# The first layer's pooling mixer: one more root, the band constants on another queue, and an order by hand for three engines

## The chip, the cores and the metric

The program runs on one core of one Trainium2 chip. The metric is device time in microseconds (us) of one execution, from start to end; three executions of the kernel before took 1045.97, 1046.10 and 1046.62 us.

## What is computed

The reference is a decoder trunk of two layers on 512 tokens of width 1024, behind which 16 learned meta rows are put in front (528 rows). Layer 0 mixes tokens by multi-scale causal pooling, layer 1 by stick-breaking attention; each layer ends with a SwiGLU network of width 2816. The change touches the pooling mixer alone:

```python
def rmsnorm(x, g):
    xf = x.astype(jnp.float32)
    y = xf * lax.rsqrt(jnp.mean(xf * xf, axis=-1, keepdims=True) + EPS)
    return (y * g.astype(jnp.float32)).astype(x.dtype)

def pool_mixer(h, w, scale):
    ...
    for g, win in enumerate(POOL_WINDOWS):          # windows 2, 4, 8, 16
        xg = hf[..., g * POOL_GROUP:(g + 1) * POOL_GROUP]
        cs = jnp.cumsum(xg, axis=1)
        lag = jnp.pad(cs[:, :-win], ((0, 0), (win, 0), (0, 0)))
        cnt = jnp.minimum(pos + 1, win).astype(jnp.float32)[None, :, None]
        outs.append((cs - lag) / cnt - xg)
    pooled = jnp.stack(outs, axis=2).astype(h.dtype)
    mixed = jnp.einsum('blgc,gcd->blgd', pooled, w).reshape(B, L, D_MODEL)
    return mixed * scale
```

## The kernel before

Matrices are held transposed, as eight chunks of 128 channels by 528 rows (`hT`). Each fp32 operand of a large matmul is split into a rounded part and the rest, so that a product is three matmuls (`mm3`, line 108): the ScalarE writes the rounded part, the VectorE subtracts.

The opening (from line 180) has four input tiles `xt[0..3]` of 128 tokens and one tile `mt` of the 16 meta rows, each 1024 wide, and goes through these steps:

- **Squares and roots.** The sum of squares of a row is made by ScalarE for tiles 0 and 2 (line 219) and by VectorE for the meta rows and tiles 1 and 3 (line 221). VectorE adds the epsilon (line 223), ScalarE takes the reciprocal root (line 137), VectorE refines it with three small operations (lines 138, 140, 141). There are two such roots: one for tiles 0, 1 and the meta rows together, one for tiles 2 and 3.
- **Split.** ScalarE writes the normalised tile rounded (`ah`, line 228), VectorE the rest (`al`, line 229), ScalarE the meta rows (`am`, line 231).
- **Bands.** The moving average is a matmul against a banded matrix. VectorE copies the constants `band_raw` into the zeroed `band` (line 232); GpSimd has set the zeros.
- **Pooling.** TensorE first runs 30 matmuls of zeros (line 238). Then it makes 16 pooled tiles: eight chunks of the first half of the rows (tiles 0 and 1 and the meta rows: lines 251, 252, 254) and eight of the second half (tiles 1, 2 and 3: six matmuls each). Each takes one of eight PSUM banks, and a bank is free for the second half only when ScalarE has written `ph` (line 257) and VectorE `pl` (line 258) from it.
- **Weights and mixing.** `pool_w` arrives in two loads and is split into `pw0`, `pw1` (lines 94 and 99). 16 products `mix` follow (line 108), each added to `hT` by VectorE (`h`, line 269). After a chunk's second half `norm.chunk` prepares the operands of the first feed-forward layer: `f0uh` and `f0sq` on ScalarE, `f0ul` and the sum of `f0sq` on VectorE.

The first feed-forward product (`pp`, line 108) takes over the PSUM banks of the opening, and waits for the last `h`. Every engine runs its instructions in one fixed order; the framework's scheduler chooses it from the order of the source and its own estimates. Loads go out on two queues: SP's (nearly all) and ScalarE's (`mt` and `gains`); a queue's loads share eight completion semaphores in turn, and SP waits before reusing one.

Of the kernel before, what the change touches and what calls it, by code (L numbers as in the profile page):

```python
# [7 lines left out]
F32 = mybir.dt.float32  # L8
F32R = mybir.dt.float32r
BF16 = mybir.dt.bfloat16  # L10
AF = mybir.ActivationFunctionType
ALU = mybir.AluOpType

P = 128
D = 1024
KC = D // P
SEQ = 512
META = 16
# [4 lines left out]
EPS = 1e-6  # L23
# [3 lines left out]
BOFF = 144  # L27
# [20 lines left out]
def f32(ap):  # L48
    return ap.bitcast(F32)
# [3 lines left out]
def trunk(ctx: ExitStack, tc: tile.TileContext, x, meta, x_t, gain, pool_w, w_qkv, w_o, w_gate, w_up, w_down,  # L53
          final_gain, c_ident, c_band, c_mband, c_mask, out):

    nc = tc.nc
# [8 lines left out]
    @contextmanager  # L65
    def phase(name, **bufs):
        with tc.tile_pool(name=name, bufs=1, space=bass.MemoryType.PSUM) as pool:
            psum["pool"], psum["bufs"] = pool, bufs
            yield

    def ps(name, tag, banks=1):

        shape = [P, 512] if banks == 1 else [P, banks, 512]
        return psum["pool"].tile(shape, F32, tag=tag, name=name, bufs=psum["bufs"][tag])
# [9 lines left out]
    def wsplit(v, name, eng=None, src=None):  # L84


        n, m = v.shape[1], v.shape[2]
        step = max(1, 512 // m)
        his, los = [], []
        for j in range(0, n, step):  # L90
            w = min(step, n - j)
            hi = main.tile([P, step, m], F32R, tag="whi", name=f"{name}h{j}", bufs=NW)[:, :w]
            lo = main.tile([P, step, m], F32R, tag="wlo", name=f"{name}l{j}", bufs=NW)[:, :w]
            nc.scalar.copy(hi, v[:, j:j + w])  # L94
            if src is not None:
                nc.scalar.activation(lo, v[:, j:j + w], AF.Copy, scale=-1.0)
                nc.gpsimd.dma_start(out=lo, in_=src[:, j:j + w], accum_op=ALU.add)
            else:
                (eng or nc.vector).tensor_tensor(out=lo, in0=v[:, j:j + w], in1=f32(hi), op=ALU.subtract)
            his += [hi[:, i] for i in range(w)]  # L100
            los += [lo[:, i] for i in range(w)]
        return his, los
# [31 lines left out]
    def rstd_of(parts, r, t):  # L134

        for ss, sl in parts:
            nc.scalar.activation(r[:, sl], ss, AF.Abs_reciprocal_sqrt, scale=1.0 / D)
        nc.vector.tensor_tensor(out=t, in0=r, in1=r, op=ALU.mult)
        for ss, sl in parts:
            nc.vector.scalar_tensor_tensor(t[:, sl], ss, -0.5 / D, t[:, sl], op0=ALU.mult, op1=ALU.mult)  # L140
        last_rstd[:] = [nc.vector.scalar_tensor_tensor(r, t, 1.5, r, op0=ALU.add, op1=ALU.mult).ins]
        return r
# [40 lines left out]
    with tc.tile_pool(name="start", bufs=1) as sp, phase("ps0", one=8):  # L183
        nc.scalar.activation(sp.tile([P, 1], F32, name="table"), ones[:, 0:1], AF.Abs_reciprocal_sqrt)
        xt = [sp.tile([P, D], F32, name=f"x{i}") for i in range(4)]
        mt = sp.tile([META, D], F32, name="mt")
        band_raw = sp.tile([P, 4, 144], F32, name="bandr")
        mband = sp.tile([P, 4, 32], F32, name="mband")
        nc.sync.dma_start(out=xt[0], in_=x[0, 0:P, :])
        nc.scalar.dma_start(out=mt, in_=meta)  # L190
        nc.sync.dma_start(out=xt[1], in_=x[0, P:2 * P, :])
        nc.scalar.dma_start(out=gains, in_=gain)
        for i in (2, 3):
            nc.sync.dma_start(out=xt[i], in_=x[0, i * P:(i + 1) * P, :])
        nc.sync.dma_start(out=band_raw, in_=c_band)
        nc.sync.dma_start(out=mband, in_=c_mband)
        pwr = [wraw(pool_w[0, :, k * P:(k + 1) * P, :].rearrange("g p d -> p g d"), f"pwr{k}") for k in range(2)]
        for c in range(KC):
            nc.sync.dma_start(out=hT[c], in_=x_t[c * P:(c + 1) * P, :])
        nc.sync.dma_start(out=consts, in_=c_ident)  # L200
        nc.sync.dma_start(out=masks, in_=c_mask)

        band = sp.tile([P, 4, BAND], F32R, name="band")
        nc.gpsimd.memset(f32(band), 0.0)
        ah = [sp.tile([P, D], F32R, name=f"ah{i}") for i in range(4)]
        al = [sp.tile([P, D], F32R, name=f"al{i}") for i in range(4)]
        am = sp.tile([P, D], F32, name="am")
        nc.gpsimd.memset(am, 0.0)
        junk = [sp.tile([P, D], BF16, name=f"junk{i}") for i in range(2)]
        rx = {}  # L210
        for part in ((0, 4, 1), (2, 3)):
            i0 = part[0]
            n = len(part)
            ss = sp.tile([P, 3], F32, name=f"ss{i0}")[:, :n]
            nc.vector.memset(ss, 1.0)
            for j, i in enumerate(part):
                src, acc = (mt, ss[:META, j:j + 1]) if i == 4 else (xt[i], ss[:, j:j + 1])
                if i in (0, 2):
                    nc.scalar.activation(junk[0], src, AF.Square, accum_out=acc)
                else:  # L220
                    nc.vector.scalar_tensor_tensor(junk[1][:src.shape[0]], src, 1.0, src, op0=ALU.mult, op1=ALU.mult,
                                                   accum_out=acc)
            nc.vector.tensor_scalar(ss, ss, D * EPS, None, op0=ALU.add)
            r = rstd_of([(ss, slice(0, n))], *[sp.tile([P, 3], F32, name=f"rx{i0}{k}")[:, :n] for k in "rt"])
            for j, i in enumerate(part):
                rx[i] = r[:, j:j + 1]
        for i in range(4):
            nc.scalar.activation(ah[i], xt[i], AF.Copy, scale=rx[i])
            nc.vector.scalar_tensor_tensor(al[i], xt[i], rx[i], f32(ah[i]), op0=ALU.mult, op1=ALU.subtract)
            if i == 1:  # L230
                nc.scalar.activation(am[:META], mt, AF.Copy, scale=rx[4][:META])
        nc.vector.tensor_copy(band[:, :, BOFF:BOFF + 144], band_raw)

        warm = sp.tile([P, 512], BF16, name="warm")
        nc.vector.memset(warm, 0.0)
        pw = ps("warm", "one")
        for _ in range(WARM):
            nc.tensor.matmul(pw, lhsT=warm[:, 0:P], rhs=warm, start=True, stop=True)

        ph, pl = [], []  # L240
        for c in range(KC):
            for dst, n in ((ph, "ph"), (pl, "pl")):
                dst.append(blk(f"{n}{c}", F32R) if c < 6 else sp.tile([P, L], F32R, name=f"{n}{c}"))
        for hf, terms in enumerate((((0, -META), (1, -144)), ((1, 120), (2, HALF - 272), (3, -136)))):
            for c in range(KC):
                g = c // 2
                cs = slice(c * P, (c + 1) * P)
                pp = ps(f"pool{c}{hf}", "one")[:, :HALF]
                for j, (i, off) in enumerate(terms):
                    rhs = band[:, g, BOFF + off:BOFF + off + HALF]  # L250
                    nc.tensor.matmul(pp, lhsT=ah[i][:, cs], rhs=rhs, start=j == 0, stop=False)
                    nc.tensor.matmul(pp, lhsT=al[i][:, cs], rhs=rhs, start=False, stop=j == len(terms) - 1)
                    if hf == 0 and j == 0:
                        nc.tensor.matmul(pp[:, 0:32], lhsT=am[:, cs], rhs=mband[:, g, :], start=False, stop=False)
                gc = gains[:, c:c + 1]
                a, b = ph[c][:, HV[hf]], pl[c][:, HV[hf]]
                nc.scalar.activation(a, pp, AF.Copy, scale=gc)
                nc.vector.scalar_tensor_tensor(b, pp, gc, f32(a), op0=ALU.mult, op1=ALU.subtract)
        pws = [wsplit(pwr[k], f"pw{k}") for k in range(2)]
        for c in range(KC):  # L260
            for hf in range(2):
                g, d = c // 2, c % 2
                pm = ps(f"mix{c}{hf}", "one")[:, :HALF]
                for k in range(2):
                    ds = slice(d * P, (d + 1) * P)
                    mm3([(pm, HV[hf])], pws[k][0][g][:, ds], pws[k][1][g][:, ds], ph[2 * g + k], pl[2 * g + k],
                        k == 0, k == 1)
                hv = hT[c][:, HV[hf]]
                nc.vector.scalar_tensor_tensor(hv, pm, gains[:, 32 + c:33 + c], hv, op0=ALU.mult, op1=ALU.add)
                if hf:  # L270
                    norm.chunk(c)
# [227 lines left out]
    with tc.tile_pool(name="att", bufs=1) as ap, phase("ps2", one=4, two=2):  # L499
        uh, ul, acc = norms[0].uh, norms[0].ul, norms[0].acc  # L500
# [4 lines left out]
        am = ap.tile([P, 4, 2 * META], F32, name="am")  # L505
# [308 lines left out]
```

## Time and profile before

| what | value |
|---|---|
| median of three executions | 1046.10 us |
| the profiled execution, its own time | 1047.39 us |
| its span, first to last instruction | 1045.6 us |
| TensorE busy | 1017.1 us, 97% |
| VectorE busy | 846.4 us, 81% |
| ScalarE busy | 550.8 us, 53% |
| GpSimd busy | 6.2 us, 1% |
| mean granted TensorE clock | 0.991 |

The profile is of one execution. Its span leaves 1.79 us of that execution's time outside. A busy time is the time in which an engine had an instruction in work; a share over the whole span says little about the opening, which is the first 4%. A row of the timeline gives start, duration, engine (PE TensorE, DVE VectorE, ACT ScalarE, POOL GpSimd), source line, operation and tiles, and in brackets how long the engine had been idle and what ended that.

### The profile page before, as it was taken

The numbers are of one execution on the slowest core, as the hardware profiler recorded it, in microseconds if no ns is written. First come the engines' busy times: TensorE is split into PE (matmuls) and PEld (weight loads), VectorE is DVE, ScalarE is ACT, GpSimd is POOL, SyncE is SP. The second block draws the span as 40 slices with busy tenths as digits, with TensorE's granted clock in tenths as the row PEclk, the third lists the DMA queues.
The fourth block names the chain that finished last, engine by engine and source line by source line (L and its number), as shares of the span: only waits on it lengthen the run. The fifth ranks groups of instructions, "written<-read, shape, count | busy, mean of one in ns | idle before, by whom it ended". The sixth has DMA issues, their size and how long they took to land.

```text
span 1045.6 us, 18479 instructions
## 1 busy us (share of the span) xinstructions
PE 1017.1 (97%) x7278; PEld 943.5 (90%) x7278; DVE 846.4 (81%) x1511; ACT 550.8 (53%) x1115; POOL 6.2 (1%) x16
## 2 busy tenths in 40 slices
PE   8999999999999999999999998999999999999996
PEld 6999999999999998988888886878999999999985
DVE  7999987888787777778888987779888777788755
ACT  7555544445545455455555455555655544445534
POOL 1000000000000010000000000000000000000000
PEclk9999999999999999999999998999999999999998
DMA  9222333333323332211111212122233323233302
GB/s 349 70 83 71 122 101 102 102 100 102 102 82 102 101 122 87 76 41 61 41 51 32 76 46 81 64 89 70 81 112 112 100 90 99 97 114 109 120 23 81
DMA packets 43112, 95.72 MB, mean 92 GB/s; under 512 B 3329, under 2 KB 20097, under 8 KB 43025
## 3 DMA queue, kind: packets, MB, share of 16 engines
q1 hardware_dynamic: 42272, 93.40, 27.2%
q8 instruction: 57, 0.93, 0.4%
q10 hardware_dynamic: 752, 1.14, 0.3%
q14 instruction: 31, 0.25, 0.1%
HBM read 92.43 MB, written 2.10 MB: 90 GB/s over the span
## 4 chain that ended last, share of the span: by engine, by line
PE 84%; DVE 11%; issue 2%; ACT 1%; DMA 1%; SPq 0%; ACTq 0%; DVEq 0%
PE pb L108 15%; PE pd L108 12%; PE pd L334 12%; PE pa L108 10%; PE pc L108 10%; PE pp L108 9%; PE pj L108 9%; DVE kp L594 2%; PE pw L108 2%; PE z L580 2%; DVE a L632 1%; PE t L607 1%; DVE sg L596 1%; PE mix L108 1%; DVE h L673 1%
## 5 line engine op out<-in xcount | busy, mean ns | idle before, releaser
L307 DVE TENSOR_TENSOR h<-pd,h 128x264 f32<-128x264 f32 x96 | 40.9, 427 | 14.9 <-PE pd L108 14.9
L594 DVE TENSOR_TENSOR_SCAN kp<-kp,estrip 128x1344 f32<-128x1344 f32 x16 | 47.3, 2954 | 3.8 <-ACT kp L589 3.4
L94 ACT CAST ws_3h<-rgate 128x512 fp32r<-128x512 f32 x36 | 22.4, 621 | 53.0 <-PE pb L108 47.8
L94 ACT CAST ws_5h<-s 128x512 fp32r<-128x512 f32 x36 | 22.4, 622 | 45.7 <-PE pb L108 33.3
L446 DVE TENSOR_TENSOR u<-pb,m 128x264 f32<-128x264 f32 (+1 forms) x36 | 15.4, 427 | 35.6 <-PE pb L108 35.5
L94 ACT CAST ws_4h<-s 128x512 fp32r<-128x512 f32 x36 | 22.4, 621 | 41.5 <-PE pa L108 24.4
L108 PE MATMUL pa<-xh,ws_0l 128*128 128x264 f32 (+1 forms) x144 | 40.9, 284 | 0.1
L108 PE MATMUL pc<-xh,ws_2h 128*128 128x264 f32 (+1 forms) x144 | 40.7, 282 | 0.3 <-ACT ws_2h L94 0.3
L108 PE MATMUL pa<-xh,ws_0h 128*128 128x264 f32 (+1 forms) x144 | 40.8, 283 | 0.0
L108 PE MATMUL pb<-xh,ws_1h 128*128 128x264 f32 (+1 forms) x144 | 40.8, 283 | 0.0
L108 PE MATMUL pb<-xh,ws_6l 128*128 128x264 f32 (+1 forms) x144 | 40.7, 283 | 0.0
L108 PE MATMUL pc<-xh,ws_2l 128*128 128x264 f32 (+1 forms) x144 | 40.7, 283 | 0.0
L108 PE MATMUL pb<-xl,ws_1h 128*128 128x264 f32 (+1 forms) x144 | 40.7, 283 | 0.0
L108 PE MATMUL pa<-xl,ws_3h 128*128 128x264 f32 (+1 forms) x144 | 40.7, 283 | 0.0
L108 PE MATMUL pb<-xh,ws_4l 128*128 128x264 f32 (+1 forms) x144 | 40.7, 283 | 0.0
L108 PE MATMUL pa<-xh,ws_3h 128*128 128x264 f32 (+1 forms) x144 | 40.7, 283 | 0.0
L108 PE MATMUL pb<-xh,ws_1l 128*128 128x264 f32 (+1 forms) x144 | 40.7, 283 | 0.0
L108 PE MATMUL pb<-xl,ws_4h 128*128 128x264 f32 (+1 forms) x144 | 40.7, 283 | 0.0
L108 PE MATMUL pc<-xl,ws_5h 128*128 128x264 f32 (+1 forms) x144 | 40.7, 282 | 0.0
L108 PE MATMUL pb<-xl,ws_6h 128*128 128x264 f32 (+1 forms) x144 | 40.7, 282 | 0.0
L108 PE MATMUL pc<-xh,ws_5h 128*128 128x264 f32 (+1 forms) x144 | 40.6, 282 | 0.0
L108 PE MATMUL pa<-xl,ws_0h 128*128 128x264 f32 (+1 forms) x144 | 40.6, 282 | 0.0
(1207 smaller groups left out, 4103.9 us busy)
## 6 DMA issues: line engine op xcount, KB each, us to landing
rgate<-in_ffn_w_gate_dram SPq DMA_DIRECT2D x44, 512.0 KB, 3.5
rup<-in_ffn_w_up_dram SPq DMA_DIRECT2D x44, 512.0 KB, 3.5
rd<-in_ffn_w_down_dram SPq DMA_DIRECT2D x42, 512.0 KB, 3.6
rq<-in_sb_w_qkv_dram SPq DMA_DIRECT2D x8, 512.0 KB, 3.4
rk<-in_sb_w_qkv_dram SPq DMA_DIRECT2D x8, 512.0 KB, 3.5
rv<-in_sb_w_qkv_dram SPq DMA_DIRECT2D x8, 512.0 KB, 3.5
rwo<-in_sb_w_o_dram SPq DMA_DIRECT2D x8, 384.0 KB, 3.0
h<-in_x_t_dram SPq DMA_DIRECT2D x8, 264.0 KB, 6.8
```

The costliest lines, as they stand in the source:

```text
L94: nc.scalar.copy(hi, v[:, j:j + w])
L108: last = nc.tensor.matmul(o, lhsT=w, rhs=xx[:, sl], start=start and i == 0, stop=stop and i == 2, skip_group_check=more)
L307: nc.vector.tensor_tensor(out=hv, in0=pd, in1=hv, op=ALU.add)
L334: nc.tensor.matmul(pd, lhsT=hid[j][x_][:, ts], rhs=w_[:, sl], start=r > 0 and i + j == 0, stop=j == len(hid) - 1 and i == 2, skip_group_ch ...
L446: tt(out=u[:, a], in0=pb, in1=m1, op=ALU.add)
L580: nc.tensor.matmul(tz[:, hd, c:c + k1 - k0], lhsT=qq[hs, i * P:(i + 1) * P], rhs=kk[hs, k0:k1], start=j == 0 and c == 0, stop=False, skip_ ...
L594: nc.vector.tensor_tensor_scan(kp[:, hd, ::-1], kp[:, hd, ::-1], estrip[:, ::-1], 1.0, op0=ALU.mult, op1=ALU.max)
L596: return nc.vector.tensor_tensor(out=sg[:, hd, 0:STRIP - 1], in0=sg[:, hd, 0:STRIP - 1], in1=kp[:, hd, 1:STRIP], op=ALU.mult).ins
L607: nc.tensor.transpose(o, sg[:, c0:c0 + n], ident)
L632: nc.vector.scalar_tensor_tensor(a0[r, i], f32(a0h[r]), lo_rows[r], p2[r, 256:384], op0=ALU.mult, op1=ALU.add)
L673: nc.vector.tensor_tensor(out=hT[c][:, TOK], in0=pj, in1=hT[c][:, TOK], op=ALU.add)
```

## The change

`band_raw` and `mband` are loaded by ScalarE's queue, behind `mt` and ahead of `gains`, not by SP's behind the tiles. GpSimd converts the band. There are three roots: tile 0 with the meta rows, tile 1, tiles 2 and 3. ScalarE and VectorE follow the written order in this part. The splits of `pool_w` are held behind the last split of a tile.

```diff
+        nc.scalar.dma_start(out=band_raw, in_=c_band)
+        nc.scalar.dma_start(out=mband, in_=c_mband)
         nc.scalar.dma_start(out=gains, in_=gain)
...
-        nc.sync.dma_start(out=band_raw, in_=c_band)
-        nc.sync.dma_start(out=mband, in_=c_mband)
...
-        nc.vector.tensor_copy(band[:, :, BOFF:BOFF + 144], band_raw)
+        nc.gpsimd.tensor_copy(band[:, :, BOFF:BOFF + 144], band_raw)
...
+        with tc.manual_schedule(engines={mybir.EngineType.Activation, mybir.EngineType.DVE}):
+            square(4, ss[0][:META, 1:2])
+            square(0, ss[0][:, 0:1], True)
+            eps(0)
+            root(0)
+            first(0)
+            square(1, ss[1])
+            eps(1)
+            square(2, ss[2][:, 0:1], True)
+            second(0)
+            root(1)
+            first(1)
+            square(3, ss[2][:, 1:2])
+            eps(2)
+            nc.scalar.activation(am[:META], mt, AF.Copy, scale=rx[4][:META])
+            second(1)
+            root(2)
+            first(2)
+            split = first(3)
+            second(2)
+            split = split, second(3)
...
-        pws = [wsplit(pwr[k], f"pw{k}") for k in range(2)]
+        with tc.issue_after(split[0]), tc.issue_after(split[1]):
+            pws = [wsplit(pwr[k], f"pw{k}") for k in range(2)]
```

`square`, `eps`, `root`, `first` (`ah`) and `second` (`al`) are the same operations as before, on one tile each; `am` is scaled by the first root.

On VectorE, in the opening, before (names: `x_83` to `x_85` are tiles 1 to 3, `al_117` to `al_120` the rests of tiles 0 to 3, `pl` the pooled rests):

```order
L223 TENSOR_SCALAR ss_137<-ss_137 128x2
L229 SCALAR_TENSOR_TENSOR al_118<-x_83,rx0r,ah_114 128x1024
L99 TENSOR_TENSOR pw0l_344<-pwr_97,pw0h_343 128x512
L99 TENSOR_TENSOR pw0l_348<-pwr_97,pw0h_347 128x512
L138 TENSOR_TENSOR rx2t<-rx2r 128x2
L99 TENSOR_TENSOR pw1l_352<-pwr_99,pw1h_351 128x512
L99 TENSOR_TENSOR pw1l_356<-pwr_99,pw1h_355 128x512
L140 SCALAR_TENSOR_TENSOR rx2t<-ss_137,rx2t 128x2
L141 SCALAR_TENSOR_TENSOR rx2r<-rx2t,rx2r 128x2
L258 SCALAR_TENSOR_TENSOR pl_192<-pool_207,gains,ph_191 128x264
L229 SCALAR_TENSOR_TENSOR al_119<-x_84,rx2r,ah_115 128x1024
L229 SCALAR_TENSOR_TENSOR al_120<-x_85,rx2r,ah_116 128x1024
```

The same place on VectorE now:

```order
L234 SCALAR_TENSOR_TENSOR al_118<-x_83,rx1r,ah_114 128x1024
L138 TENSOR_TENSOR rx2t<-rx2r 128x2
L140 SCALAR_TENSOR_TENSOR rx2t<-ss_128,rx2t 128x2
L141 SCALAR_TENSOR_TENSOR rx2r<-rx2t,rx2r 128x2
L234 SCALAR_TENSOR_TENSOR al_119<-x_84,rx2r,ah_115 128x1024
L234 SCALAR_TENSOR_TENSOR al_120<-x_85,rx2r,ah_116 128x1024
L99 TENSOR_TENSOR pw0l_354<-pwr_97,pw0h_353 128x512
L99 TENSOR_TENSOR pw0l_358<-pwr_97,pw0h_357 128x512
L99 TENSOR_TENSOR pw1l_362<-pwr_99,pw1h_361 128x512
L99 TENSOR_TENSOR pw1l_366<-pwr_99,pw1h_365 128x512
L283 SCALAR_TENSOR_TENSOR pl_202<-pool_217,gains,ph_201 128x264
```

The four weight splits moved from ahead of the last two tile splits to behind them, and the first `pl`, which frees the first bank, moved from ahead of them to behind all of these; ScalarE's rows move in the same way.

On VectorE at the end of the mixer, before (`h_73` is the last chunk of `hT`):

```order
L155 SCALAR_TENSOR_TENSOR f0ul_444<-h_69,gains,f0uh_443 128x528
L269 SCALAR_TENSOR_TENSOR h_72<-mix_504,gains,h_72 128x264
L269 SCALAR_TENSOR_TENSOR h_73<-mix_519,gains,h_73 128x264
L269 SCALAR_TENSOR_TENSOR h_73<-mix_527,gains,h_73 128x264
L155 SCALAR_TENSOR_TENSOR f0ul_467<-h_70,gains,f0uh_466 128x528
```

And now:

```order
L155 SCALAR_TENSOR_TENSOR f0ul_454<-h_69,gains,f0uh_453 128x528
L295 SCALAR_TENSOR_TENSOR h_72<-mix_506,gains,h_72 128x264
L295 SCALAR_TENSOR_TENSOR h_72<-mix_514,gains,h_72 128x264
L295 SCALAR_TENSOR_TENSOR h_73<-mix_529,gains,h_73 128x264
L155 SCALAR_TENSOR_TENSOR f0ul_477<-h_70,gains,f0uh_476 128x528
L295 SCALAR_TENSOR_TENSOR h_73<-mix_537,gains,h_73 128x264
```

One `f0ul` more stands ahead of the last `h`. Behind this place all engines have the rows of before in the order of before.

## Rows read from the trace of the kernel before

**Rows 1.** Waits of TensorE, 0 to 60 us: total, times, longest.
```profile
PE pp L108 <- DVE h L269: 1.6, 1, 1.6
```

**Rows 2.** Timeline of all engines, opening: start, us, engine, line, operation, tiles.
```profile
1.35 8.96 PE L238 MATMUL warm<-warm 128*128 128x512 bf16 x30 [1.35 <-DVE warm L235]
4.95 1.06 ACT L219 ACTIVATE junk<-x 128x1024 bf16<-128x1024 f32 x1 [2.26 <-DMA x<-in_x_dram]
5.91 0.19 ACT L219 ACTIVATION_READ_ACCUMULATOR junk<-x 128x1 f32 x1
6.37 1.22 DVE L221 SCALAR_TENSOR_TENSOR junk<-x 128x1024 bf16<-128x1024 f32 x1 [0.94 <-DMA x<-in_x_dram]
...
7.71 0.17 DVE L223 TENSOR_SCALAR ss<-ss 128x3 f32<-128x3 f32 x1
...
8.15 0.16 DVE L138 TENSOR_TENSOR rx0t<-rx0r 128x3 f32<-128x3 f32 x1 [0.27 <-ACT rx0r L137]
...
8.54 0.16 DVE L141 SCALAR_TENSOR_TENSOR rx0r<-rx0t,rx0r 128x3 f32<-128x3 f32 x1
...
10.03 0.46 DVE L232 CAST band<-bandr 128x576 fp32r<-128x576 f32 x1
...
11.14 1.14 ACT L231 ACTIVATE am<-mt,rx0r 16x1024 f32<-16x1024 f32 x1
11.60 0.17 DVE L223 TENSOR_SCALAR ss<-ss 128x2 f32<-128x2 f32 x1
```

**Rows 3.** Timeline further, from the weight splits to the first feed-forward product.
```profile
12.87 1.29 DVE L99 TENSOR_TENSOR pw0l<-pwr,pw0h 128x512 fp32r<-128x512 f32 x2
...
15.73 2.19 ACT L228 ACTIVATE ah<-x,rx2r 128x1024 fp32r<-128x1024 f32 x2 [0.63 <-DVE rx2r L141]
...
16.92 2.48 DVE L229 SCALAR_TENSOR_TENSOR al<-x,rx2r,ah 128x1024 fp32r<-128x1024 f32 x2 [0.80 <-ACT ah L228]
...
19.31 2.89 DVE L258 SCALAR_TENSOR_TENSOR pl<-pool,gains,ph 128x264 fp32r<-128x264 f32 x7
...
19.86 0.59 PE L251 MATMUL pool<-band,ah 128*128 128x264 f32 x1
...
26.39 0.28 PE L252 MATMUL pool<-band,al 128*128 128x264 f32 x1
26.51 0.28 PE L108 MATMUL mix<-ph,pw0h 128*128 128x264 f32 x1
...
34.78 0.49 DVE L269 SCALAR_TENSOR_TENSOR h<-mix,gains,h 128x264 f32<-128x264 f32 x1 [0.21 <-PE mix L108]
...
39.78 0.76 DVE L155 SCALAR_TENSOR_TENSOR f0ul<-h,gains,f0uh 128x528 fp32r<-128x528 f32 x1
...
40.02 0.48 PE L108 MATMUL pp<-f0uh,wgate0h 128*128 128x264 f32 x2 [1.63 <-DVE h L269]
```

**Rows 4.** TensorE by stretch: length, busy (instructions), clock, DMA; last row: timeline.
```profile
19.00:20.00 1.00, 0.54 (x2) 0.86 1.02 406
23.00:24.00 1.00, 1.00 (x10) 0.94 1.06 410
647.00:648.00 1.00, 0.00 (x0) 0.88 0.00 0
654.00:655.00 1.00, 1.00 (x4) 0.70 0.00 0
...
649.40 2.37 PE L607 MATMUL t<-consts,sg 128*128 128x128 f32 x10 [3.59 <-DVE sg L596]
```

**Rows 5.** DMA issue (KB, us to landing), and all engines, clock, DMA share, GB/s.
```profile
bandr<-in_c_band_dram SPq DMA_DIRECT2D x1, 288.0 KB, 7.1
...
15.00:20.00 5.00, 3.38 (x23) 2.67 (x21) 4.17 (x8) 4.26 (x9) 0.00 (x0) 0.97 1.06 387
```

**Rows 6.** Timeline of GpSimd and of VectorE at 380 us.
```profile
380.86 1.01 POOL L509 CAST a<-am 128x128 fp32r<-128x128 f32 x4
...
381.74 0.69 DVE L99 TENSOR_TENSOR wq0l<-rq,wq0h 128x512 fp32r<-128x512 f32 x1
```

More of the change, by code (lines that the diff above doesn't have):

```diff
@@ L209, in trunk @@
         junk = [sp.tile([P, D], BF16, name=f"junk{i}") for i in range(2)]
[L210 to L231, printed above, removed]
-        nc.vector.tensor_copy(band[:, :, BOFF:BOFF + 144], band_raw)
+        nc.gpsimd.tensor_copy(band[:, :, BOFF:BOFF + 144], band_raw)
+        ss = {i: sp.tile([P, n], F32, name=f"ss{i}") for i, n in ((0, 2), (1, 1), (2, 2))}
@@ new lines, in trunk, with square @@
+        rt = {i: [sp.tile([P, t.shape[1]], F32, name=f"rx{i}{k}") for k in "rt"] for i, t in ss.items()}
+        nc.vector.memset(ss[0], 1.0)
+        rx = {0: rt[0][0][:, 0:1], 4: rt[0][0][:, 1:2], 1: rt[1][0][:, 0:1], 2: rt[2][0][:, 0:1], 3: rt[2][0][:, 1:2]}
+        def square(i, acc, on_act=False):
+            src = mt if i == 4 else xt[i]
+            if on_act:
+                nc.scalar.activation(junk[0], src, AF.Square, accum_out=acc)
+            else:
+                nc.vector.scalar_tensor_tensor(junk[1][:src.shape[0]], src, 1.0, src, op0=ALU.mult, op1=ALU.mult,
+                                               accum_out=acc)
@@ new lines, in eps, with root, first, second @@
+        def eps(i):
+            nc.vector.tensor_scalar(ss[i], ss[i], D * EPS, None, op0=ALU.add)
+        def root(i):
+            return rstd_of([(ss[i], slice(0, ss[i].shape[1]))], *rt[i])
+        def first(i):
+            return nc.scalar.activation(ah[i], xt[i], AF.Copy, scale=rx[i]).ins
+        def second(i):
+            return nc.vector.scalar_tensor_tensor(al[i], xt[i], rx[i], f32(ah[i]), op0=ALU.mult,
+                                                  op1=ALU.subtract).ins
+        with tc.manual_schedule(engines={mybir.EngineType.Activation, mybir.EngineType.DVE}):
[19 more added lines that the diff above has]
+            split = split, second(3)
```

## The prediction

> **What bounds the kernel now.** I read the waits of TensorE first, because TensorE is busy for 97% of the span and only its gaps and slow stretches can be won or lost. In the first 60 us the longest wait is the one ahead of the first feed-forward product: 1.6 us until VectorE's last addition to `h` [rows 1]. From 40.02 on TensorE runs through, and behind the mixer the order of every engine is unchanged. So one number carries the whole effect: when does that first product start, at 40.02 now [rows 3]? Whatever it moves, the end moves.
>
> Next I read the timeline of the opening backwards from there. In the rows the reader is to see that VectorE, not TensorE, sets the pace. TensorE is held by its 30 matmuls of zeros until 1.35 + 8.96 = 10.31 [rows 2], so nothing pooled can start earlier whatever the roots do. The second half of pooling waits for the last two tile splits on VectorE, which run 16.92 to 19.31, and its second chunk starts at 19.86, when the bank is free [rows 3]. Mixing starts at 26.51 and the last additions end just before 40.02.
>
> Last I read the clock. In the stretch from 19 to 20 us the granted clock is 0.86, from 23 to 24 us 0.94 [rows 4]. With two levels, 2.4 and 1.2 GHz, it fell at about 19.72 and rose at about 23.12; ahead of the fall TensorE had been busy for 3.38 of the 5 us from 15 to 20 [rows 5], with its gaps late in them (0.54 of the last one). From 19.86 to 26.51 there are 7 chunks of 6 matmuls in 6.65 us. At the full clock one of this shape starts 0.12 us behind the other (26.39, 26.51) [rows 3], so 42 would take 5.1 us: **1.55 us** are lost to the half clock, in 3.25 us, 0.48 for each us.
>
> **The change, part by part.** I walk along VectorE and ScalarE in the new order.
>
> *Load queue.* The first tile lands for the square at 4.95 [rows 2]. The band, 288 KB, now travels beside the tiles instead of behind them. At the 387 GB/s of a busy stretch [rows 5] this is 0.76 us if all of it goes first, and nothing if it goes behind. I take 0.3 us, since tile 0 is issued first and mostly gone by then; ends 0 and 0.76. Later tiles are later by more, but VectorE and ScalarE come to them later too. SP loses two issues of its queue; what follows still waits for semaphores and gains nothing. If the band or `mband` lands late, TensorE's first half waits, which has over 2 us of cover (below): nothing.
>
> *Roots.* The square of tile 0 ends with its readout at 6.10 [rows 2], with the delay 6.40. Before, the epsilon came at 7.71, behind tile 1's square on VectorE. From epsilon to the factor takes 7.71 to 8.70, 0.99 us: factor at 7.4. Then VectorE does: square of tile 1, 6.37 to 7.71 with what follows, 1.34; epsilon and `al` of tile 0, 11.60 to 12.87, 1.27; three root operations, 8.15 to 8.70, 0.55 [rows 2, 3]. That is 10.56. The same three pieces again for tile 3's square, tile 1's `al` and the last root: 3.16, so **13.72**. Before, the last root was ready at 15.7. The third root thus costs 0.99 us of VectorE and ScalarE, half of it on the path; the band's copy, 0.46 us, leaves VectorE [rows 2].
>
> *Last splits.* From the start of `ah` to the start of `al` is 15.73 to 16.92, 1.19; the two `al` take 2.39 to the next operation at 19.31 [rows 3]. 13.72 + 1.19 + 2.39 = 17.3, against 19.31 before: 2.0 us are won here.
>
> *Weights behind them.* The four splits of `pool_w` are not saved, only moved: 2 x 1.29 = 2.58 us [rows 3], now between the last `al` and the first `pl`. 17.3 + 2.58 = 19.9, and the first `pl` (0.49) ends at **20.4**. The second half's first chunk needs that bank. Before, this `pl` was done early, and this chunk was complete when 19.86 came. So the 2.0 us are given back, and TensorE begins 8 chunks at 20.4 where it began 7 at 19.86.
>
> *TensorE.* `am` now stands behind tile 1's `ah`: 10.56 + 1.1 + 1.14 = 12.8, against 12.28 [rows 2]. Behind it TensorE has 24 matmuls of the first half left, 2.9 us at 0.12 each and some 4.5 if the short ones with `am` take several times as long, as an estimate; so it is done between 15.7 and 17.3 and idle for **3 us or more** until 20.4. Eight chunks are 48 x 0.121 = 5.8 us at the full clock. I take the same loss to the half clock as now, 1.55: mixing starts at 27.75, **1.25 us later**. The ends: no loss, 26.2; or the price of the longer hold. After the wait of 3.59 us at 649.40 the clock fell at about 647.76 and rose at about 654.6 [rows 4], so 5.2 us of work ran at half speed: 2.5 us, mixing at 28.7, 2.2 us later.
>
> *From mixing to the first product.* Now 26.51 to 40.02. One more `f0ul` stands ahead of the last `h`: 39.78 to the next operation, about 0.68 us; against it a gap of 0.21 us in which VectorE waited for TensorE [rows 3] closes. **+0.45 us** (0.2 to 0.7).
>
> The sum: 1.25 + 0.45 = **+1.7 us**. The profiled execution took 1047.39, so it would take 1049.1; the median of the three is 1046.10, so by the same shift **1047.8**.
>
> **The rivals.** *The clock is held low for longer* (slower). For it: the new gap, 3 us or more, is like the 3.59 us at 649.40, where half clock lasted 6.8 us, and unlike the partly busy stretch before 19.72, where it lasted 3.4 [rows 4]. Against: work resumes later after the fall the longer the gap, so the second stretch may be shorter. 2.2 + 0.45 = +2.65: 1048.7. It decides where TensorE's work at 20.4 is too little for the clock to rise before about 23.
>
> *VectorE and GpSimd hold each other up* (slower). GpSimd now reads `band_raw` at about 6 to 9 us, while VectorE squares tile 1 and splits tile 0, with two operands each. If one of these had to wait for GpSimd's whole conversion, all of the chain behind is late. GpSimd's conversion of 128 elements takes 1.01 / 4 = 0.25 us [rows 6]; 576 elements lie between 0.25 (all fixed) and 1.14 (all by size). I take 0.9, nearer to the latter, since four times 0.25 shows no more than a small operation. 1.7 + 0.9 = +2.6: 1048.7. The trace's only pair speaks mildly against: the VectorE subtraction at 381.74 starts 0.13 us before GpSimd's last conversion ends and takes the usual 0.69. By the Trainium skill, page "SBUF — State Buffer", section "Who interferes with whom", a VectorE instruction with two SBUF inputs and a GpSimd instruction that reads SBUF exclude each other for the whole instruction, and the one that starts second waits. By that rule, whichever is ready first decides, the sum is this rival's whenever GpSimd gets in between two of VectorE's operations; the pair at 381.74 bears neither way for longer than 0.13 us.
>
> *The clock never falls, or the loss hides.* Then mixing could start at 26.2, but VectorE is the bound: from 19.9 it has 16 `pl` (2.89 / 7 = 0.41 each) and four feed-forward weight splits, 6.6 + 2.6 = 9.1, until 29.0 against about 28.3 before, and it makes up the idle 0.2 to 1 us of the stretch after. +0 to +0.7: 1046.4. Against it: a gap of 3 us, with a fall after less.
>
> *Faster by more.* It would need the order to hide the weight splits beside other VectorE work, which the rows don't show; even tile 0 earlier by 1.3 us buys TensorE only 0.33 us (10.64 to 10.31), and that is covered. About 1043.5.
>
> **How the numbers follow.** The forecast (+1.7) 0.49; clock held longer 0.21; GpSimd in the way 0.21; no loss 0.05; faster 0.04. A measurement of this kernel can tell 0.2%, 2.1 us, from no change. The forecast and the case without loss lie within it: 0.54. The two slow rivals lie beyond it, at +2.6: 0.42. Faster: 0.04. The range: from no loss with the tile not late, 1046.1, to both slow rivals in part, 1049.2.
>
> **What would show it.** In the new trace: first pooled matmul at 10.3, waiting for nothing but the zeros; `al` of tile 3 ending near 17.3; four `pw` splits behind it; first `pl` ending near 20.4 (0.3 less if tile 0 isn't late); TensorE idle ahead of that for 3 us; half clock after it; mixing at 27.7; first feed-forward product at 41.7. I am wrong if the last `al` ends after 18.5 (look for a VectorE operation stretched or late beside GpSimd's), if the half clock lasts past 24, if VectorE rather than TensorE is behind at the last `h`, or if the stretch behind 42 us is not the old one shifted.

## The result: slower by 0.5%, where the prediction held no change the likeliest

The changed kernel took 1052.11 us (median of four executions, 1050.02 to 1053.16), the kernel before 1046.03 beside it: ratio 1.0052, 95% interval 1.0035 to 1.0068. Forecast were 1047.8, with 1049.2 as the upper end. The profiled execution took 1053.16 us, 5.8 more than that of before, and its span is longer by the same 5.8 (1051.4 against 1045.6). Its mean granted clock is 0.986; before it was 0.991.

The opening first, in the order in which the prediction walked it. Timeline of the changed kernel (start, us, engine, line, operation, tiles, in brackets the idle time ahead and what ended it):

```profile
5.08 1.06 ACT L219 ACTIVATE junk<-x 128x1024 bf16<-128x1024 f32 x1 [2.40 <-DMA x<-in_x_dram]
...
7.17 1.22 DVE L221 SCALAR_TENSOR_TENSOR junk<-x 128x1024 bf16<-128x1024 f32 x1
...
7.48 1.43 POOL L210 CAST band<-bandr 128x576 fp32r<-128x576 f32 x1 [4.00 <-DMA bandr<-in_c_band_dram]
...
8.53 1.46 DVE L234 SCALAR_TENSOR_TENSOR al<-x,rx0r,ah 128x1024 fp32r<-128x1024 f32 x1
...
11.70 1.27 DVE L234 SCALAR_TENSOR_TENSOR al<-x,rx1r,ah 128x1024 fp32r<-128x1024 f32 x1
...
13.28 0.16 DVE L141 SCALAR_TENSOR_TENSOR rx2r<-rx2t,rx2r 128x2 f32<-128x2 f32 x1
13.47 2.19 ACT L231 ACTIVATE ah<-x,rx2r 128x1024 fp32r<-128x1024 f32 x2 [0.71 <-DVE rx2r L141]
14.65 2.48 DVE L234 SCALAR_TENSOR_TENSOR al<-x,rx2r,ah 128x1024 fp32r<-128x1024 f32 x2 [1.22 <-DMA h<-in_x_t_dram]
17.05 1.28 DVE L99 TENSOR_TENSOR pw0l<-pwr,pw0h 128x512 fp32r<-128x512 f32 x2
18.26 1.28 DVE L99 TENSOR_TENSOR pw1l<-pwr,pw1h 128x512 fp32r<-128x512 f32 x2
19.46 0.88 DVE L283 SCALAR_TENSOR_TENSOR pl<-pool,gains,ph 128x264 fp32r<-128x264 f32 x2
...
20.00 0.59 PE L276 MATMUL pool<-band,ah 128*128 128x264 f32 x1 [3.29 <-DVE pl L283]
```

The last `al` ends near 17.05 instead of 19.31 [rows 3], the four weight splits follow it, the first `pl` is done when TensorE goes on at 20.00, and TensorE has waited 3.29 us for it. (The `al` row at 14.65 names a load of `h` as what ended the wait. `al` reads no `h`; the first of its two `ah`, which it does read, was done at about 14.6.) TensorE's waits in the first 60 us, where the longest of before was 1.6 us [rows 1]:

```profile
PE pool L276 <- DVE pl L283: 3.3, 1, 3.3
PE pp L108 <- DVE h L295: 2.0, 1, 2.0
```

And the clock by stretch. Columns: length, busy time (instructions) of PE, PEld, DVE, ACT, POOL, granted clock, DMA share, GB/s:

```profile
15.00:20.00 5.00, 1.71 (x15) 1.50 (x14) 5.00 (x8) 5.00 (x12) 0.00 (x0) 0.90 1.06 386
20.00:25.00 5.00, 5.00 (x22) 5.00 (x23) 5.00 (x12) 4.11 (x9) 0.00 (x0) 0.50 1.03 409
25.00:30.00 5.00, 5.00 (x39) 5.00 (x39) 3.96 (x9) 2.41 (x5) 0.00 (x0) 0.91 0.67 238
40.00:45.00 5.00, 3.00 (x18) 2.82 (x16) 5.00 (x10) 5.00 (x9) 0.00 (x0) 0.79 0.01 3
45.00:50.00 5.00, 5.00 (x38) 5.00 (x38) 4.85 (x8) 0.95 (x3) 0.00 (x0) 0.87 0.03 3
420.00:425.00 5.00, 4.48 (x29) 3.39 (x30) 1.10 (x2) 4.34 (x6) 0.00 (x0) 0.68 0.34 108
```

The same places in the kernel before (here and from now on without the columns of PEld to POOL):

```profile
20.00:25.00 5.00, 5.00 (x30) 0.69 1.03 407
...
40.00:45.00 5.00, 4.99 (x41) 1.00 0.02 3
...
415.00:420.00 5.00, 3.36 (x32) 1.00 0.34 108
420.00:425.00 5.00, 5.00 (x48) 1.00 0.00 0
```

With two levels, 2.4 and 1.2 GHz, a clock of 0.90 over 5 us is 2 x 0.10 x 5 = 1.0 us at the lower one. So the opening has 6.9 us at half clock, where before it had some 3.4; there are 3.4 more from 40 to 50 us, and 3.2 more at 420. Before, neither of these two places shows a fall, though TensorE has a gap at the second of them too (3.36 of 5 us busy). The landmarks that follow, first a row of before, then three rows of the changed kernel:

```profile
49.59 1.05 PE L175 MATMUL fb0p<-f0sq,ones 128*128 128x264 f32 x4
```

```profile
28.55 0.28 PE L108 MATMUL mix<-ph,pw0h 128*128 128x264 f32 x1
...
42.42 0.48 PE L108 MATMUL pp<-f0uh,wgate0h 128*128 128x264 f32 x2 [2.00 <-DVE h L295]
...
53.49 0.83 PE L175 MATMUL fb0p<-f0sq,ones 128*128 128x264 f32 x3
```

Mixing starts 2.04 us later than before (26.51, [rows 3]), the first feed-forward product `pp` 2.40 later (40.02), the norm's broadcast `fb0p`, 9.6 us of work further, 3.90 later. So the fall behind `pp` is worth 1.5 us. The fall at 420 is worth 1.5 us more at the 0.48 us for each us that the prediction read from rows 3 and 4. That is 5.4 of the 5.8.

### The profile page after: what moved, and what is told of

Same layout as the page of the kernel before. It is cut to its first block, busy times and chain, and to the rows that moved or that the text cites. A ratio compares the mean times of both kernels' runs of the same rounds, so it can differ in the third digit from the quotient of the medians.

```text
span 1051.4 us, 18484 instructions
## 1 busy us (share of the span) xinstructions
PE 1020.3 (97%) x7278; PEld 947.5 (90%) x7278; DVE 847.1 (81%) x1513; ACT 551.1 (52%) x1116; POOL 7.7 (1%) x17
## 4 chain that ended last, share of the span: by engine, by line
PE 84%; DVE 11%; issue 2%; ACT 1%; DMA 1%; SPq 0%; ACTq 0%; DVEq 0%
PE pb L108 15%; PE pd L108 12%; PE pd L360 12%; PE pa L108 10%; PE pc L108 10%; PE pp L108 9%; PE pj L108 9%; DVE kp L620 2%; PE pw L108 2%; PE z L606 2%; DVE a L658 1%; PE t L633 1%; DVE sg L622 1%; DVE h L699 1%; PE po L672 1%
## 5 line engine op out<-in xcount | busy, mean ns | idle before, releaser
L333 DVE TENSOR_TENSOR h<-pd,h 128x264 f32<-128x264 f32 x96 | 40.8, 426 | 14.9 <-PE pd L108 14.9
```

Of the source, the lines that this page charges most:

```text
L333: nc.vector.tensor_tensor(out=hv, in0=pd, in1=hv, op=ALU.add)
```

## The experiments

Theory A: the hold of the weight splits (TensorE idle for 3.3 us, clock down behind it) and the one `f0ul` that the scheduler puts ahead of the last `h` cost the time. Rival B: the third root, the other queue and GpSimd's conversion do. All ratios are to the kernel before, run beside on the same chip, and stand with their 95% interval; they rest on 5 to 12 executions of each version and 17 to 35 of the kernel before.

### Which part of the change: e1, e2, e3

e1 is the changed kernel without the hold:

```diff
-        with tc.issue_after(split[0]), tc.issue_after(split[1]):
-            pws = [wsplit(pwr[k], f"pw{k}") for k in range(2)]
+        pws = [wsplit(pwr[k], f"pw{k}") for k in range(2)]
```

Without the hold the scheduler also leaves the fifth `f0ul` behind the last `h`, as before the change.

> The changed kernel without the hold on the weight splits: the four splits of pool_w are again scheduled among the roots, and two of the pooled rests stand ahead of the last two tile splits. Theory A (the held weight splits leave TensorE without a free bank for 3.3 us at 16.7 us, and the clock stays low for 6.8 us): the gap breaks up into waits of about 1 us or less, mixing starts at 26 to 27 instead of 28.6, the first feed-forward product at 40 to 41 instead of 42.4; 1045 to 1048 us. Theory B (the third root, the queue or GpSimd's conversion costs the time): the time stays at 1050 to 1053.

e2 is the kernel before with the loads of the bands on ScalarE's queue and `nc.gpsimd.tensor_copy` for `nc.vector.tensor_copy`:

> The kernel before, with only the band constants moved to ScalarE's queue and the band converted by GpSimd; roots and orders are those of before. Theory A: VectorE loses 0.46 us of work ahead of the tile splits, the tiles land up to 1 us later; first feed-forward product at 39.7 to 40.5, 1045.5 to 1047 us. Theory B (bands): tiles or VectorE late by more than 1 us, 1048 us or more.

e3 is the kernel before with the hold alone (the two lines that e1 takes out, put in behind the last `ah` and `al`); the scheduler then sets the extra `f0ul` too:

> The kernel before, with only the hold of the weight splits behind the last tile split; two roots, bands as before. The scheduler then also puts one f0ul more ahead of the last h, as in the changed kernel. Theory A: the whole loss comes with this one edit: TensorE idle for 3 us or more until about 20, half clock for 6.8 us, mixing at 28.5, 1050 to 1053 us. Theory B: 1046 to 1047.

Measured: e1 1045.65 us, 0.9994 (0.9984 to 1.0004). e2 1046.78, 1.0000 (0.9992 to 1.0009). e3 1050.42, 1.0042 (1.0026 to 1.0057). So the hold with what the scheduler made of it brings nearly all of the loss by itself, and without it the third root, the queue and GpSimd cost nothing that can be measured, which is to say less than about 1 us. B falls. (e2's expectation was missed in one point: in its profile `pp` starts at 40.81, 0.79 us later than before, since tile 1's square begins 0.50 us later and the epsilon behind it takes 0.43 us instead of 0.17.) In e1 the opening runs at full clock:

```profile
15.00:20.00 5.00, 3.74 (x27) 1.00 1.06 389
20.00:25.00 5.00, 5.00 (x42) 1.00 1.02 405
```

Mixing starts at 24.52 and `pp` at 38.05 there, 2.0 us ahead of before. Yet the median is no better by more than the interval, and its executions lie from 1043.23 to 1047.70. One cause can be seen in the profile, a fall at 417 us that before lacks:

```profile
415.00:420.00 5.00, 4.99 (x36) 0.69 0.32 108
```

But work that no version touches differs as well. Two stretches further on, first before, then e1:

```profile
645.00:655.00 10.00, 6.41 (x25) 0.66 0.17 52
685.00:695.00 10.00, 10.00 (x37) 0.83 0.24 71
```

```profile
645.00:655.00 10.00, 6.40 (x29) 0.83 0.17 52
685.00:695.00 10.00, 10.00 (x45) 1.00 0.32 99
```

There the kernel before has 10.2 us at half clock and e1 3.4. At 641 us e1 is 0.43 us ahead of before, at the second norm's broadcast `fb1p` (695.57 before, 692.85 in e1) 2.72. Of the 16 profiles of all versions ten have 10.2 us near 650 and 690 us and six 3.4 (e1, e3, e9, e11, e12, e13). So some 2.3 us of an execution's time are decided here, in work that no edit touches, and no single profile's time tells what an edit of the opening is worth.

### Another place for the weights: e4

The changed kernel, with the weight splits held behind the last `ph` and `pl` of the first half instead.

```diff
+                if hf == 0 and c == KC - 1:
+                    split = ev
```

Here `ev` is the pair of evictions of that chunk.

> The changed kernel with the weight splits held still further, behind ScalarE's and VectorE's reading of the last pooled tile of the first half. VectorE frees banks right after the last tile split at 17.1, so TensorE goes on at about 17.6 after a gap near 1 us and the weight splits stand beside its second half. Theory A: half clock for 3.4 us or not at all, mixing at 24.5 to 26.5, first feed-forward product at 39 to 40.5; 1044.5 to 1047 us, the best of the orders. Theory B: 1050 or more.

Measured: 1047.48, 1.0008 (0.9999 to 1.0018). Mixing started at 23.84, 2.7 us ahead of before, but the wait ahead of `pp` was 3.0 us instead of 1.6, and the clock fell there. `pp` started at 38.74, only 1.3 us ahead, and `fb0p` at 49.83, 0.24 behind: VectorE's arrears took back about one half of what the opening won, and the fall the rest.

### The changed kernel once more: e0

> The changed kernel itself, once more, beside the next three on one chip. If the three falls of the granted clock that its first profile shows and the kernel before lacks (longer hold at 19 us, one at 42 us, one at 420 us) belong to the order of the work, they stand here again and the time is about 1052 (1050 to 1053). If a fall is partly chance, the profile will lack one or two of them, and the times of its executions will lie in steps of about 1.6 us, what 3.4 us at half clock costs.

Measured: 1051.04 (1047.99 to 1053.35), 1.0047 (1.0032 to 1.0061). The loss stands, but its falls don't: this profile has 3.4 us at half clock in the opening, none at 42 us although the wait ahead of `pp` is 1.97 again, and a fall at 419.

```profile
15.00:20.00 5.00, 1.78 (x16) 0.96 1.06 390
20.00:25.00 5.00, 4.93 (x29) 0.70 1.02 405
...
40.00:45.00 5.00, 3.75 (x31) 1.00 0.01 3
```

In four profiles of the same opening (the changed kernel twice, e7 and e13, both below) the half clock lasted 6.9, 3.4, 3.4 and 10.2 us. In the first three the clock fell in the long wait or just behind it, at 19.0 to 21.0 us; in e13 it fell at 14.9, ahead of that wait and some 2 us behind one of 1.1 us for `am`:

```profile
15.00:20.00 5.00, 3.12 (x16) 0.50 1.06 389
```

One profile doesn't tell what a wait costs in clock; the spread of the executions does.

### The extra `f0ul`: e7, e8

e7 is the changed kernel with VectorE's order at the end of the mixer as before, e8 the kernel before with only that order changed. Both write this order out as a table; the diff is that of e7's table against one that gives the changed kernel's order:

```diff
-        (7, 0): 'u4', (7, 1): 's3 u5 u6 s4 u7 s5 s6 s7'
+        (7, 0): '', (7, 1): 'u4 s3 u5 u6 s4 u7 s5 s6 s7'
```

The key is chunk and half of the `h` behind which they stand, `u4` the fifth `f0ul`, `s3` the fourth of the sums of `f0sq`. e8 goes the other way in the kernel before.

> The changed kernel with VectorE's order at the end of the mixer as before: the fifth f0ul behind the last h instead of ahead of it. The wait ahead of the first feed-forward product should be 1.3 to 1.6 us instead of 2.0. Theory A2 (the extra f0ul makes the second fall of the clock): first product 0.45 us earlier and no fall there, together about 2 us: near 1050. Rival (the fall at 42 us comes from the longer low clock ahead, not from the wait of 2.0): only the 0.45 us, near 1051.6, the fall stays.

> The kernel before, with one f0ul more ahead of the last h and nothing else of the change. Its direct price is 0.42 us (first product at 41.25 against 40.83 in two runs that differ in this alone). Theory A2 (a wait of 2.0 us ahead of the first product, instead of 1.6, lets the clock fall there or later in more of the executions): about 2 to 3 us above the kernel before, 1.002 to 1.003, with steps of 1.6 us between executions. Rival (the weights' hold and the extra f0ul are needed together): only the 0.42 us, ratio 1.0004.

Measured: e7 1047.93, 1.0011 (1.0003 to 1.0020); e8 1048.20, 1.0016 (1.0005 to 1.0027). In the changed kernel the place of one operation of 0.76 us is worth 3.1 us (1051.04 to 1047.93; near 1050 was expected), in the kernel before 1.6 (1048.20 to 1046.63). What e7 still loses, 1.3 us, is left to the hold. The direct price of that operation is smaller. From the start of mixing to `pp` e0 takes 13.88 us and e7 13.20, e8 14.21 and the kernel before 13.51: 0.7 us either way, about the length of the operation. (The 0.42 us that e8's expectation takes from the starts of `pp`, 41.25 and 40.83, is too small, since e7's mixing starts 0.26 us later than e0's.) The table fixes VectorE's order alone, and ScalarE's moves a little with it; e9 below has that order of ScalarE and the extra `f0ul`, and takes 13.88 as e0 does, so it is VectorE's order that counts. The rest comes behind `pp`. In e8's profile, first the wait, then the clock:

```profile
PE pp L110 <- DVE h L284: 2.3, 1, 2.3
```

```profile
40.00:45.00 5.00, 4.22 (x22) 0.66 0.01 3
...
420.00:425.00 5.00, 5.00 (x33) 0.66 0.33 108
```

In e7's the wait is 1.3, and both places are at full clock:

```profile
PE pp L110 <- DVE h L310: 1.3, 1, 1.3
```

```profile
40.00:45.00 5.00, 4.17 (x34) 1.00 0.01 3
...
420.00:425.00 5.00, 5.00 (x48) 1.00 0.06 20
```

Over all 16 profiles the fall behind `pp` goes with the wait ahead of it, though not always: with waits of 0.7 to 1.6 us there is none in nine profiles (in five of them zeros shorten the wait), with waits of 2.0 us or more there is one in five of seven (after, e4, e5, e8, e9; not e0 and e3, both 2.0).

### The waits kept, the clock held up: e5, e6, e9, e10, e13

If the clock is the cost, TensorE need only be given something to do in the waits. e5 puts 28 matmuls of zeros into the opening wait, e6 17 more into the wait ahead of `pp`. VectorE's order is pinned to that of the changed kernel.

```diff
+                if hf == 1 and c == 0:
+                    for _ in range(28):
+                        with tc.issue_after(last):
+                            last = nc.tensor.matmul(full[:, 272:512], lhsT=warm[:, 0:P], rhs=warm[:, 0:240], start=True,
+                                                    stop=True, skip_group_check=True).ins
```

> The changed kernel with 28 matmuls of zeros of 240 columns (about 0.1 us each) in TensorE's wait of 3.3 us ahead of the second half of pooling, into unused columns of a bank; VectorE's order is as in the changed kernel. Theory A (the wait costs mainly by the half clock behind it): the first second-half matmul still starts at about 20.0, but mixing starts near 26 instead of 28.55 and the first feed-forward product near 40.5 instead of 42.4; time about 2 us below the changed kernel, near 1050. Rival (the wait itself, VectorE's order behind it): mixing earlier, but the first product stays at 42.0 to 42.4, time unchanged within 0.5 us.

> The same, and 17 matmuls of zeros more in the wait of 2.0 us ahead of the first feed-forward product. Theory A: no fall at 42 us either, so 1.5 us less between the first product and the norm's broadcast (9.7 instead of 11.2), time near 1048.5. If the fall at 42 was an accident of that one execution, the time is that of the kernel with the first filling alone. If the fall at 420 us hangs on how the opening went, it goes too: near 1047.

Measured: e5 1055.61, 1.0079 (1.0062 to 1.0096), e6 1053.49, 1.0070 (1.0058 to 1.0082). The filling missed the wait. It wrote into the bank of chunk 7, whose `ph` and `pl` stand behind the weight splits, and waited for them:

```profile
20.93 5.54 PE L290 MATMUL pool<-warm 128*128 128x240 bf16 x28 [4.10 <-DVE pl L304]
```

So e5 has the wait, the low clock and 5 us of zeros on top, and says nothing on theory A; the part of e6 at the end of the mixer worked (clock 1.00 from 40 to 50 us), but the two intervals overlap and what it is worth can't be read from the two.

e9 mends this: 30 matmuls go into the bank of chunk 5, ahead of that chunk's own five, which nothing has read yet. e10 adds the 17 at the end, e13 has these alone.

```diff
-            for c in range(KC):
+            if hf == 0:
+                tiles = [ps(f"pool{c}0", "one") for c in range(KC)]
+            for c in (range(KC) if hf else (0, 1, 2, 3, 4, 6, 7, 5)):
...
+                if hf == 0 and c == 5:
+                    for _ in range(30):
```

> The filling of the opening wait, mended: 30 matmuls of zeros of 240 columns go into the bank of chunk 5, ahead of that chunk's own five matmuls, so that they wait for no pl; they run from about 16.2 to 19.2 and chunk 5 behind them to about 20.1. Clock theory: no fall at 19 us, second half of pooling from 20.0 at full clock, mixing near 26 to 26.5 instead of 27.4 to 28.5, first product about 1 to 1.5 us earlier (VectorE is close to being the bound); the wait of 2.0 ahead of it stays, and may be longer. Time 1049.5 to 1050.5 where the changed kernel has 1051 to 1052. Rival (VectorE is the bound, the half clock is hidden): unchanged, 1051 to 1052.

> The same, and 17 matmuls of zeros in the wait ahead of the first product, with the extra f0ul where the changed kernel has it. If the clock is what the extra f0ul costs beyond its 0.42 us, the time is some 2 us below that of the opening filling alone, near 1048, although the last h is as late. If the order itself costs, it stays near 1050.

> The changed kernel, with hold and extra f0ul, and 17 matmuls of zeros in the wait of 2.0 us ahead of the first product. If the extra f0ul costs 3 us there (1051.0 against 1047.9 where it is undone) because the clock falls behind that wait, nearly all of it comes back: 1048 to 1048.5. If the order of VectorE itself costs, the time stays at 1051.

Measured: e9 1048.48, 1.0015 (1.0003 to 1.0027); e10 1047.42, 1.0006 (0.9998 to 1.0015); e13 1048.96, 1.0026 (1.0018 to 1.0035). e9's filling, and its clock in the opening:

```profile
16.06 3.25 PE L294 MATMUL pool<-warm 128*128 128x240 bf16 x30
```

```profile
15.00:20.00 5.00, 5.00 (x48) 1.00 1.06 387
20.00:25.00 5.00, 5.00 (x42) 1.00 1.02 407
```

Mixing starts at 25.92, before its time in the kernel before. The wait of 2.0 us ahead of `pp` is still there in e9, and the clock fell behind it:

```profile
40.00:45.00 5.00, 5.00 (x30) 0.66 0.00 0
```

With the hold and the extra `f0ul` where the change has them, zeros in the first wait bring back 2.6 us (1051.04 to 1048.48), in the second 2.1 (to 1048.96), in both 3.6 (to 1047.42), of a loss of 4.4 (the kernel before stood at 1046.3 to 1046.6 beside each). The intervals of e9 and e10 lie clear of e0's (1.0032 to 1.0061); e13's touches it, so the 2.1 is the least sure of the three. The useful work was left as it was (only chunk 5 of the first half now comes last), and the zeros at the end even cost time of their own: with them mixing to `pp` takes 14.3 us (e10, e13) instead of 13.9, as the last `h` waits for them. This is the strongest ground for the clock as the cost.

### A version without both causes: e11, e12

e11: no hold, the weights' low parts on GpSimd, the order of e7 at the end, 14 matmuls of zeros ahead of `pp`. e12: the same with the low parts on VectorE. Of e11's edit, the part that the versions above don't have:

```diff
-        with tc.issue_after(split[0]), tc.issue_after(split[1]):
-            pws = [wsplit(pwr[k], f"pw{k}") for k in range(2)]
+        pws = [wsplit(pwr[k], f"pw{k}", nc.gpsimd) for k in range(2)]
```

> The changed kernel with its hold removed, the low parts of the pool weights made by GpSimd instead of VectorE, the fifth f0ul behind the last h, and 14 matmuls of zeros in the wait ahead of the first product. The first pl stands right behind the last al: TensorE should go on at about 17.6 after a wait of 1 us, mixing start near 24, the first product near 38, no fall of the clock in the opening. Against the kernel before 2 to 3 us less, ratio 0.9975. If GpSimd's four subtractions hold VectorE's operations up, or come later than 24, mixing is late and the time is that of the kernel before.

> The changed kernel with the weights' splits not held, the fifth f0ul behind the last h, and 14 matmuls of zeros in the wait ahead of the first product. Both causes found so far are gone: mixing near 24.5, first product near 38, no fall of the clock before 400 us. The version without the filling and with its own tail stood at 0.9994 of the kernel before; if the waits ahead of the first product bring falls later on, this is a little better, 0.998 to 0.999. If it is 0.9994 again, the opening's 2 us are given back by falls that no edit of the opening governs.

Measured: e11 1049.25, 1.0024 (1.0016 to 1.0033); e12 1046.13, 0.9998 (0.9988 to 1.0008). Both were expected to be faster than the kernel before; neither is. e11 shows what the prediction's second rival feared. GpSimd, then VectorE:

```profile
13.32 2.51 POOL L101 TENSOR_TENSOR pw0l<-pwr,pw0h 128x512 fp32r<-128x512 f32 x2 [4.35 <-ACT pw0h L96]
15.80 2.50 POOL L101 TENSOR_TENSOR pw1l<-pwr,pw1h 128x512 fp32r<-128x512 f32 x2
```

```profile
13.90 0.72 DVE L140 TENSOR_TENSOR rx2t<-rx2r 128x2 f32<-128x2 f32 x1 [0.86 <-ACT rx2r L139]
14.66 1.20 DVE L142 SCALAR_TENSOR_TENSOR rx2t<-ss,rx2t 128x2 f32<-128x2 f32 x1
15.89 1.19 DVE L143 SCALAR_TENSOR_TENSOR rx2r<-rx2t,rx2r 128x2 f32<-128x2 f32 x1
```

Three root operations of two columns, 0.16 us each elsewhere in the same trace, took 0.72, 1.20 and 1.19: each ended within 0.06 us of the end of one of GpSimd's subtractions of 1.25 us. The last root came at 17.1 instead of 13.4, and mixing at 28.84 (in this profile the clock was also low from 14.7 us on, for 10.2 us). In e12's profile the clock was low from about 15 us on for 6.8 us, against its expectation, and between the 30 matmuls of zeros and that fall TensorE had no longer wait than 1.2 us for `am`. No version beats the kernel before by more than can be told.

## Why the prediction failed, step by step

**Load queue, roots, last splits, weights: held.** The square came 0.13 us late, where 0.3 was taken. The last root was done at 13.44 (13.72 forecast), the last `al` at 17.05 (17.3), TensorE went on at 20.00 (20.4) after 3.29 us ("3 us or more"). The walk along VectorE, made from durations of the trace before and the new order, was right within 0.4 us at each mark.

**GpSimd in the way: the two do lock each other out, but the size was small.** By the Trainium skill, page "SBUF — State Buffer", section "Who interferes with whom", a VectorE instruction with two SBUF inputs and a GpSimd instruction that reads SBUF lock each other out, and the later waits. e11 agrees: 0.72 to 1.20 us where 0.16 is usual, each ending with one of GpSimd's operations. In the changed kernel it was mostly GpSimd that came second: its conversion starts at 7.48 and ends at 8.91, in e13 it starts at 7.90 and ends at 8.86, in both 0.52 us behind the end of VectorE's square of tile 1, so most of the 1.43 us is a wait for that square. `al` of tile 0 behind it took 1.46 instead of 1.27: 0.19 us, with 0.9 given to this rival. e2, which has the conversion and the queue alone, is level with before.

**From mixing to the first product: the direct price held.** +0.45 was forecast, 0.68 for the `f0ul` less a gap that closes; it was 0.36 in the first profile and 0.37 in e0's. The `f0ul` alone is 0.7 by e7 and by e8, so the gap closes by about 0.3.

**TensorE: the term that failed.** "I take the same loss to the half clock as now, 1.55." The half clock lasted 6.9 us in the first profile: mixing at 28.55, not 27.75. The rival of the longer hold named this, 28.7, and had 0.21. But in e0's profile the low clock lasted 3.4 us again and the kernel's median was still 1051.04, so this alone is not it; and that rival's 1048.7 lies 3.4 us below the measured time.

**"Whatever it moves, the end moves": the step that cost most.** The rest behind 42 us was taken as the old one shifted. It was not: a wait of 2.0 instead of 1.6 us ahead of `pp` was priced at its 0.4 us, not as a place where the clock may fall. It is worth 3.1 us by e7, of which 0.7 is the direct price, and about 2 by e13. In the first profile the fall behind it cost 1.5 us and the one at 420 as much again. "From 40.02 on TensorE runs through" is wrong as a reading, too: the trace of before has gaps further on, 1.64 us in the stretch from 415 to 420 and the 3.59 us at 649 that the prediction itself uses [rows 4]. The prediction named "if the stretch behind 42 us is not the old one shifted" among what would make it wrong, and gave it no chance and no price. (In the rival without loss 6.6 + 2.6 is 9.2, not 9.1, which changes nothing.)

How much is the clock in all? Each execution has its mean granted clock, so (1 - clock) x 2 x span is its time at the lower level. Means over the executions:

| kernel | executions | mean clock | at half clock, us | mean time, us |
|---|---|---|---|---|
| before (beside e0) | 17 | 0.9925 | 15.6 | 1046.59 |
| e0, the change | 6 | 0.9883 | 24.5 | 1051.02 |
| e3, hold in the kernel before | 6 | 0.9892 | 22.7 | 1050.89 |
| e7, tail order undone | 11 | 0.9913 | 18.3 | 1047.74 |
| e9, opening filled | 12 | 0.9918 | 17.3 | 1048.51 |
| e10, both filled | 12 | 0.9932 | 14.3 | 1047.35 |

The changed kernel has 8.9 us more at half clock. At 0.48 us each that is 4.3 of the 4.4 us. Between executions of one and the same kernel the time rises by only about 0.32 us for each us so worked out (the clock is given to three places, and some half clock falls where TensorE waits, as at 647 to 648 us [rows 4]); by that it is 2.8. So by this estimate the clock is between two thirds and nearly all of the loss. What is left, up to 1.6 us, is the direct cost. e0's profile agrees: with no more half clock in the opening than before, its mixing starts 0.86 us later than before and its `pp` 1.23.

**What stays open.** The fall at 415 to 425 us. It stands in all seven profiles in which `pp` had waited about 2.0 us or more (the change twice, e3, e4, e5, e8, e9), but also in four of the nine with a shorter wait (e1, e11, e12, e13), not in before, e2, e6, e7 and e10. The stretch itself is the same work in all. Whether the opening sets it, and how, wasn't found, nor what decides between 3.4 and 10.2 us at half clock near 650 and 690 us. Why one and the same opening has half clock for 3.4, 6.9 or 10.2 us is open too. And how the loss divides between the two waits is known only within the intervals above.

## What to carry to other kernels

Price a new wait of TensorE by more than its length: where the trace of before shows the clock falling after waits of that size, it needs a chance and a price of its own, at every place where a wait grows, also where it grows by 0.4 us only. Holding back work that fills an engine's gaps (here weight splits that ran while VectorE waited for a root) moves it in front of whatever comes next; compare the new order of the whole stage, since the scheduler may move an operation 20 us further that matters more, as here. And a cause that acts by chance from execution to execution is measured by many executions of a kernel with the cause taken away, not by the difference of two profiles.

## What was not expected of the hardware

- The same program's clock differs from execution to execution: with one and the same opening, 3.4 to 10.2 us at half clock, and times in a range of 5 us (1047.99 to 1053.35). Work that no edit touched takes part: 10.2 or 3.4 us at half clock near 650 and 690 us, a difference worth about 2.3 us.
- Zeros in a wait paid here: 30 matmuls of zeros in 3.25 us brought 2.6 us, those in both waits 3.6, though they compute nothing.
- Three of VectorE's smallest operations suffered far more beside GpSimd than a large one: in e11 0.16 us became 1.20, nearly GpSimd's own 1.25, while in the changed kernel GpSimd's conversion of 576 columns mostly waited itself and cost VectorE's `al` 0.19 us.
